# Norm factors folded into the split operands, side work paced by operand readiness, and the last two heads split on chip, in a two-layer hybrid decoder step

## The chip, the core and the metric

The kernel runs on one core of a Trainium2 chip. The metric is device time in microseconds, the median of three runs; lower is better. Durations in the text come from one profiled execution of the kernel before. Its engines are written as in the profile: PE (matrix products; PEld its weight loads), DVE (VectorE), ACT (ScalarE), POOL (GpSimd) and SP (which issues the weight loads from memory).

## The reference, cut to what matters

One inference step of two layers over 560 columns of tokens (16 meta tokens, 512 prompt tokens, 8 samples of 4 tokens), model width 1024. Each layer is a token mixer and a gated feed-forward part.

```python
h = rmsnorm(x, g_pre_mix)               # x * r * g, r = rsqrt(mean(x*x) + eps): one factor per token
z = h @ w_in                            # one projection into u | xb | gb | q | k | v | gc | gates a, b, c
y_a = s5_mixer(u)                       # complex diagonal scan, gelu, GLU
y_b = rglru_mixer(xb, gb)               # conv, block gates, linear scan, times gelu(gb)
y_c = retention_mixer(q, k, v, gc)      # 8 heads, rotary q and k, chunked decay, norm per head, times silu(gc)
m = sigmoid(ga) * (y_a @ w_branch_a) + sigmoid(gb) * (y_b @ w_branch_b) + sigmoid(gc) * (y_c @ w_branch_c)
x = x + rmsnorm(m @ w_out, g_post_mix)
h = rmsnorm(x, g_pre_ffn)
g, u = split(h @ ffn_w_up)
x = x + rmsnorm((gelu(causal_conv(g)) * u) @ ffn_w_down, g_post_ffn)
```

All is float32. The norm's factor r is one number per token, so it may be multiplied into h or into each product that h has been through.

## The kernel before, in words

**Products.** Activations stand transposed: 128 rows of a feature block by 560 token columns, in two column halves of 280 (`HS`). Each operand is held as a pair, a rounded part (`hi`) and the remainder (`lo`), and a product is three matmuls per block of 128 rows: hi·hi, hi·lo, lo·hi (`half`). A weight chunk of 128 output features is eight blocks: 24 matmuls per half, 48 per chunk. Weights come by SP from memory as `wr`, ACT casts them to `wh`, DVE subtracts for `wl`.

**The norm, deferred.** The split operands `hh`/`hl` (the list `hs`) hold x·g without r. r (`rn`, `N["r"]`) is ready only later, so every product is scaled when its PSUM tile is read: `by_column` (a DVE multiply by `rn`) for u, xb, gb, gc and the gates ta, tb, tc; the rotary tables `cosT` and `sinT` (tile `cst`) are multiplied by `rn` instead of k and q; v has its tokens on the partitions and is scaled by `rtok` on ACT. For gb, gc and the gates the multiply is done in place in PSUM and ACT reads the result.

**Order of the work.** The program writes its own order. A main line of weight chunks runs on PE: u and k, then per pair of heads `hp` q, v, gc and the units xb, gb of the LRU branch, then six gates tc, then the product bc of the heads' outputs, and so on. Beside it run generators of side work (S5, LRU, retention `ret_gen`, loads with splitting `load_split`), whose instructions are slipped into the main line by `pump` in the middle and at the end of each half, when a clock kept by the program (`clk`, class `Paced`) says that they are due; `finish` drains one generator before the main line goes on. The engines execute in order, so an instruction slipped in too early blocks what is queued behind it. All activations share 46 tiles of 128 x 560 (`slot`, `NG`), and a generator goes on only if enough are free.

**The end of retention.** Each head's output is stored to memory (`ycd`) on POOL's queue by `ret_gen`. Before the product bc, the main line drains the last pair of heads, then starts `load_split` over all eight heads (load as `y`, cast to `yh` on ACT, remainder `yl` on DVE) and drains it:

```python
box = [gate("tc") for _ in range(NTC)]
flush()
finish(ret, "ret")
yl = start(load_split(ycd, ych, 0.5))
finish(yl, "yl")
```

POOL issues all DMAs but the weights' and a few at the start. It also does small powers (`le`, `dt`, `E` of the preparation of S5 and LRU; `rn` of retention's norm) and memsets.

Of the kernel before, what the change touches and what calls it, by code (L numbers as in the profile page):

```python
# [18 lines left out]
D = 1024  # L19
# [63 lines left out]

@with_exitstack
def tile_hybrid_decoder(ctx: ExitStack, tc: tile.TileContext, I, O, cfg=None):
# [4 lines left out]
    clk = dict(V=0.0, A=0.0, G=0.0, P=0.0, D=0.0, set=None, used=0.0)  # L90
    SETS = {AF.Tanh: (1, 2), AF.Exp: (3, 1), AF.Gelu_apprx_tanh: (2,), AF.Ln: (3,), AF.Sqrt: (4,)}

    class Paced:
# [5 lines left out]
        def __getattr__(self, name):  # L99
            f, key = getattr(self.engine, name), self.key  # L100

            def call(out, *a, **k):
                if name == "preload_act_table_set":
                    if clk["set"] != 3:
                        clk["set"] = 3
                        clk["A"] = max(clk["A"], clk["P"]) + 1.3
                        f(out)
                    return
                n = 1
                for d in out.shape[1:]:  # L110
                    n *= d
                if key == "P":
                    src = k["rhs"] if name == "matmul" else out
                    clk["P"] += n * (0.42e-3 if src.dtype == FR else 1.7e-3) + 0.005
                elif key == "D":
                    clk["used"] = max(clk["used"], max(clk["P"], clk["V"], clk["A"]) + 2.5)
                else:
                    if key == "A":
                        c = 0.1 + n * 0.83e-3
                        if name == "activation":  # L120
                            t = SETS.get(a[1], ())
                            if t and clk["set"] not in t:
                                c += 1.3
                                clk["set"] = t[0]
                    elif key == "V":
                        c = 0.07 + n * (6.4e-3 if name == "reciprocal" else 1.04e-3)
                    else:
                        c = 0.1 + n * (165e-3 if k.get("op") == OP.pow else 1e-3)
                    clk[key] = max(clk[key], clk["P"]) + c
                    clk["used"] = max(clk["used"], clk[key])  # L130
                return f(out, *a, **k)  # L131
            return call

    V, A, G, P, SP, SQ = (Paced(e, k) for e, k in ((nc.vector, "V"), (nc.scalar, "A"), (nc.gpsimd, "G"), (nc.tensor, "P"), (nc.sync, "D"),
                                                  (nc.gpsimd, "D")))
# [27 lines left out]
    def pad_tile(name):  # L163
        return gen.tile([128, 592], FT, name=nm(name), tag="pad", bufs=3)

    def main_ps():
        return pm.tile([128, 512], FT, name=nm("pm"), tag="m", bufs=4)

    def side_ps(tag="x"):
        return pm.tile([128, 512], FT, name=nm("px"), tag=tag, bufs=2)  # L170
# [67 lines left out]
    def issue_raw(upto):  # L238
        while st["raw"] <= min(upto, len(chunks) - 1):
            i = st["raw"]  # L240
            src = chunks[i][1]
            n = src.shape[-1]
            if NRAW <= i < NRAW + BOOT:
                raws[i] = [(slot("wr")[:, :512], slice(o, o + 512)) for o in (0, 512)]
            else:
                raws[i] = [(ring.tile([128, 1024], FT, name=f"wr{i}", tag="raw", bufs=NRAW)[:, :n], slice(0, n))]
            for t, sl in raws[i]:
                SP.dma_start(t, src[:, sl])
            st["land"] = landed[i] = max(max(clk["P"], clk["V"]) + 3.8, st["land"] + 2.0)
            st["raw"] += 1  # L250
# [8 lines left out]
    def issue_hi():  # L259
# [10 lines left out]
        hi = pool.tile([128, 1024], FR, name=f"wh{i}", tag="hi" + x, bufs=b)  # L270
        lo = pool.tile([128, 1024], FR, name=f"wl{i}", tag="lo" + x, bufs=b)
# [37 lines left out]
    side = []  # L309

    SLACK, DEEP, SHALLOW = cfg.get("slack", 0.6), cfg.get("deep", 6.0), cfg.get("shallow", 1.0)
# [26 lines left out]

    def pump():
# [10 lines left out]
        for s in sorted([s for s in side if not s[4]], key=lambda s: s[2]):  # L350
            if (s in side and s[1] <= clk["P"] and used["n"] + s[3] <= NG
                    and max(clk["V"], clk["A"]) - clk["P"] < (st["shallow"] if s[2] else DEEP)):
                step(s)

    def force(but=None):

        for s in sorted(side, key=lambda s: (s[2], s[1])):
            if s is not but and used["n"] + s[3] <= NG:
                step(s)
                return  # L360
        assert False, ("no room", used["n"])

    def room(n):
        while used["n"] + n > NG:
            assert not used["side"]
            force()

    def finish(s, what=""):
        if cfg.get("verbose"):
            print("finish", what, s in side, "chunk", st["next"], "t", clk["P"], clk["V"], clk["A"], used["n"], flush=True)  # L370
        while s in side:
            t = min((t for t in side if t is s or t[2] and s[2]), key=lambda t: t[1])
            clk["P"] = max(clk["P"], t[1])
            if used["n"] + t[3] > NG:
                force(t)
# [271 lines left out]
    def by_column(N, h, out, ps, cols=None):  # L647

        until(N, "ready", h)
# [147 lines left out]
    def s5_gen(l, sp, p, ud, zd, qt):  # L797
# [162 lines left out]
        for n in range(12):  # L960
# [40 lines left out]
            for j, t in enumerate((hr, hi)):  # L1001
                G.memset(k3(t)[:, :, 8:9], 0.0)
# [153 lines left out]
    def ret_gen(l, hp, T, ycd, rp, before):  # L1156
# [172 lines left out]
        for h in range(2):  # L1329
# [10 lines left out]
            yield 0  # L1340
            SQ.dma_start(ycd[hd], sg)
            drop()
# [45 lines left out]
    def k_or_q(T, n, hs):  # L1388
        def ev(h, ps):
            if n not in T:  # L1390
                T[n] = slot(n + "f")
            A.copy(T[n][:, HS[h]], ps)
        return (n, lambda: hs, ev, None)

    def first_units(N, ud, T, between, lead):

        us = u_units(N, ud) + [k_or_q(T, "k", N["hs"])]
# [89 lines left out]
    for l in range(depth):  # L1487
# [3 lines left out]
        with ExitStack() as ph:  # L1491
            sp = ph.enter_context(tc.tile_pool(name=f"s5p{l}", bufs=1))

            def hslot(name):
                return sp.tile([128, 288], FT, name=nm(name), tag="q", bufs=NQ)
# [21 lines left out]
            for t in (cosT, sinT):  # L1517
                tt(t, t, N["r"])
# [8 lines left out]
            def lru_units(j):  # L1527
# [11 lines left out]
                unit("xb", hs, lambda h, ps: pad_evac(xp, ps, h, 3, N), go)  # L1539
# [9 lines left out]
            nl = 0  # L1549
            for hp in range(4):  # L1550
                T = TT[l] if hp == 0 else {}
                in_turn([k_or_q(T, n, hs) for n in ("k", "q") if n not in T])
                (i0, w0), (i1, w1) = weights("v"), weights("v")
                flush()
                ret = start(ret_gen(l, hp, T, ycd, rp, ret))
                T["v"] = []
                for c0 in (0, 2, 4):
                    ps = main_ps()
                    for c in range(c0, min(c0 + 2, 5)):
# [11 lines left out]
                        if c % 2 == 1 or c == 4:  # L1571
                            def ev(ps=ps, c0=c0, c1=c, T=T):
                                T["v"].append(slot("v"))
                                for i in range(c1 - c0 + 1):
# [7 lines left out]
                T["sg"] = []  # L1582
                for h2 in range(2):
                    box = {}

                    def ev(h, ps, box=box):
# [6 lines left out]
                    unit("gc", hs, ev, lambda T=T, box=box: T["sg"].append(box["t"]))  # L1593
# [4 lines left out]
            def gate(n, new=slot):  # L1598
                box = {}

                def ev(h, ps):
# [5 lines left out]
                    by_column(N, h, ps, ps)  # L1607
# [8 lines left out]
            def load_split(srcs, out, scale=None):  # L1616
                for src in srcs:
                    yield 3
                    t = slot("y")
                    SQ.dma_start(t, src)  # L1620
                    yield 2
                    a, b = slot("yh", FR), slot("yl", FR)
# [4 lines left out]
            st["shallow"] = cfg.get("sh1", 6.0)  # L1627
# [46 lines left out]
        with ExitStack() as ph:  # L1674
# [63 lines left out]
            drop(17)  # L1738
# [4 lines left out]
        with ExitStack() as ph:  # L1743
# [4 lines left out]
            if not last:  # L1748
                SQ.dma_start(cst[:, CO["cos"][0]:CO["cos"][0] + 2 * NT], I["cst"][:, CO["cos"][0]:CO["cos"][0] + 2 * NT])
# [329 lines left out]
```

## Time and profile before

| | before |
|---|---|
| median of 3 runs | 2341.22 us (2339.77 to 2342.35) |
| the profiled execution | 2338.64 us, span 2336.9 us, mean granted clock 0.99 |
| PE busy | 2273.8 us (97%), 17880 matmuls |
| DVE busy | 1664.4 us (71%) |
| ACT busy | 937.3 us (40%) |
| POOL busy | 317.6 us (14%) |

The profiled execution's own time is a little above its span, because the span runs from the first to the last instruction. A table by stages gives for each engine the microseconds it was busy; what is missing to the length of the stage is idle time. PEclk is the granted share of TensorE's full 2.4 GHz. A wait is put down to the instruction that released it.

### The profile page before, as it was taken

Reading aid. Unit: us, or ns where it says so; the run is one execution under the profiler, and the core shown is the slowest. Engines: PE = TensorE matmul, PEld = TensorE weight load, DVE = VectorE, ACT = ScalarE, POOL = GpSimd, SP = SyncE. Lnnn points to the kernel's source line nnn. Section 1 sums busy time; section 2 is a strip of 40 time slices with the busy share of each in tenths; the row PEclk is TensorE's granted clock in tenths of the full one; section 3 lists DMA queues with packets and bytes.
Section 4 is the critical chain, followed back from the end, with each engine's and each line's share of the span. In section 5 each row is a group of like instructions: output and inputs, shape, how many; then the busy total and the mean of one; then the engine's idle time right before and its main releaser. Section 6 shows DMA issues by size and latency. Waiting matters only on the chain.

```text
span 2336.9 us, 44994 instructions
## 1 busy us (share of the span) xinstructions
PE 2273.8 (97%) x17880; PEld 2253.0 (96%) x17880; DVE 1664.4 (71%) x4025; ACT 937.3 (40%) x2035; POOL 317.6 (14%) x585
## 2 busy tenths in 40 slices
PE   8999998999999999999999999979999999999997
PEld 7999998999999999999999999979999999999997
DVE  7888999887466845555588889888874667455555
ACT  4255536443435432223333455464434354332231
POOL 2222112011110000000241322110111100000011
PEclk9999999999999999999999999989999999999998
DMA  5333334233344332223342333332334433322331
GB/s 192 110 106 110 100 92 132 90 108 97 111 125 132 95 106 82 88 85 90 116 129 91 115 117 95 92 121 91 107 90 116 125 123 99 111 88 85 91 108 55
DMA packets 76707, 246.35 MB, mean 105 GB/s; under 512 B 13712, under 2 KB 16656, under 8 KB 76496
## 3 DMA queue, kind: packets, MB, share of 16 engines
q1 hardware_dynamic: 52704, 175.98, 25.0%
q0 software_dynamic: 23792, 67.49, 9.2%
q8 instruction: 141, 2.31, 0.4%
q14 instruction: 70, 0.57, 0.1%
HBM read 208.81 MB, written 29.76 MB: 102 GB/s over the span
## 4 chain that ended last, share of the span: by engine, by line
PE 65%; DVE 17%; issue 10%; ACT 4%; POOL 2%; DMA 2%; SPq 0%; POOLq 0%; DVEq 0%; ACTq 0%
PE pm L131 61%; PE px L131 4%; DVE wl L131 3%; DVE r L131 2%; ACT wh L131 1%; DVE ltr L131 1%; DVE pm L131 1%; DVE tg L131 1%; DVE cm L131 1%; POOL rn L131 1%; DVE sg L131 1%; DVE xc L131 1%; DMA wr<-in_wa 1%; DVE S L131 1%; DVE CA L131 1%
## 5 line engine op out<-in xcount | busy, mean ns | idle before, releaser
L131 ACT CAST wh<-wr 128x1024 fp32r<-128x1024 f32 (+3 forms) x347 | 347.3, 1004 | 509.9 <-PE pm L131 429.8
L131 DVE TENSOR_TENSOR wl<-wr,wh 128x1024 fp32r<-128x1024 f32 (+3 forms) x347 | 403.6, 1165 | 133.2 <-ACT wh L131 132.4
L131 PE MATMUL pm<-fh,wh 128*128 128x280 f32 (+2 forms) x1632 | 481.1, 295 | 10.4 <-ACT tg L131 4.5
L131 PE MATMUL pm<-mh,wh 128*128 128x280 f32 (+2 forms) x1664 | 483.2, 290 | 1.1 <-DVE gp L131 0.6
L131 PE MATMUL pm<-ml,wh 128*128 128x280 f32 (+2 forms) x1664 | 482.6, 290 | 0.0
L131 PE MATMUL pm<-mh,wl 128*128 128x280 f32 (+2 forms) x1664 | 482.1, 290 | 0.0
L131 PE MATMUL pm<-fh,wl 128*128 128x280 f32 (+2 forms) x1632 | 475.5, 291 | 0.0
L131 PE MATMUL pm<-fl,wh 128*128 128x280 f32 (+2 forms) x1632 | 475.4, 291 | 0.0
L131 PEld LDWEIGHTS pm<-fh,wh 128*128 128x128 f32 x1632 | 309.5, 190 | 12.9 <-ACT tg L131 4.8
L131 PEld LDWEIGHTS pm<-mh,wh 128*128 128x128 f32 x1664 | 313.1, 188 | 2.1 <-issue 0.9
L131 PEld LDWEIGHTS pm<-ml,wh 128*128 128x128 f32 x1664 | 312.7, 188 | 0.3
L131 PEld LDWEIGHTS pm<-mh,wl 128*128 128x128 f32 x1664 | 312.8, 188 | 0.0
L131 PEld LDWEIGHTS pm<-fl,wh 128*128 128x128 f32 x1632 | 309.4, 190 | 0.3
L131 PEld LDWEIGHTS pm<-fh,wl 128*128 128x128 f32 x1632 | 309.1, 189 | 0.0
L131 PE MATMUL pm<-hh,wh 128*128 128x280 f32 x928 | 276.1, 298 | 12.1 <-ACT hh L131 6.8
L131 PE MATMUL pm<-hh,wl 128*128 128x280 f32 x928 | 271.1, 292 | 1.3 <-DVE wl L131 1.3
L131 PE MATMUL pm<-hl,wh 128*128 128x280 f32 x928 | 271.3, 292 | 0.1
L131 PEld LDWEIGHTS pm<-hh,wh 128*128 128x128 f32 x928 | 175.3, 189 | 14.5 <-ACT hh L131 9.1
L131 PEld LDWEIGHTS pm<-hh,wl 128*128 128x128 f32 x928 | 175.4, 189 | 1.9 <-DVE wl L131 1.9
L131 PEld LDWEIGHTS pm<-hl,wh 128*128 128x128 f32 x928 | 175.0, 189 | 0.8 <-DVE hl L131 0.6
L131 PE MATMUL pm<-yh,wh 128*128 128x280 f32 (+2 forms) x448 | 133.9, 299 | 8.7 <-ACT yh L131 8.7
L131 PE MATMUL pm<-yl,wh 128*128 128x280 f32 (+2 forms) x448 | 131.5, 294 | 0.6 <-DVE yl L131 0.6
(363 smaller groups left out, 4229.3 us busy)
## 6 DMA issues: line engine op xcount, KB each, us to landing
wr<-in_wa SPq DMA_DIRECT2D x249, 512.0 KB, 3.6
wr<-in_w SPq DMA_DIRECT2D x44, 384.0 KB, 3.0
wr<-in_wd SPq DMA_DIRECT2D x32, 448.0 KB, 3.3
wr<-in_wd SPq DMA_DIRECT2D x16, 512.0 KB, 3.6
ycd<-sg POOLq DMA_DIRECT2D x16, 280.0 KB, 2.8
y<-ycd POOLq DMA_DIRECT2D x16, 280.0 KB, 5.4
ss<-in_rets POOLq DMA_DIRECT2D x16, 256.0 KB, 3.4
out_rets<-ss POOLq DMA_DIRECT2D x16, 256.0 KB, 2.6
```

Source lines behind the costliest of these rows:

```text
L131: return f(out, *a, **k)
```

## The change

1. **Norm factors into the operands.** A new generator `normalize` is started for each half as soon as r is known. For each of eight blocks POOL adds hi and lo into a spare tile and multiplies by r; when the products that still need the unscaled operands are past (`free[h]`), ACT casts the result into `hi` in place and DVE subtracts into `lo`. u, the first k, q, v and gc stay with unscaled operands. From the first LRU unit on, all PSUM tiles are read without the factor. The rotary tables are no longer scaled and no longer loaded again for the second layer.
2. **Pacing.** The program's clock now follows operands: each tile has the times at which it is made and last read, each instruction starts when its engine, its inputs and its output are free, and buffers that are reused carry their times over (`turn`, `cells`, `place`). The slack of a step falls from 0.6 to 0.3, the depth allowed in the gates' stretch from 6.0 to 3.0, and slots wanted by the pair of heads in work are reserved (`spare`).
3. **Heads.** The first six heads are loaded while the last pair is in work, up to three at a time; the last two are split where they are made, with no store and load.
4. A memset of two columns in S5 goes from POOL to DVE.

```diff
+                t = max(t, clk[e])
+                clk[e] = t + c
+                m[s] = t + c + lat
+                clk["used"] = max(clk["used"], t + c + lat)
...
+    def spare(s=None):
+        h = next((t for t in side if t in heads), None)
+        return h[3] if h is not None and h is not s else 0
...
     def by_column(N, h, out, ps, cols=None):
+        if N is None:
+            A.copy(out, ps)
+            return
...
-                G.memset(k3(t)[:, :, 8:9], 0.0)
+                V.memset(k3(t)[:, :, 8:9], 0.0)
...
-            yield 0
-            SQ.dma_start(ycd[hd], sg)
-            drop()
+            if straight is None:
+                yield 0
+                SQ.dma_start(ycd[hd], sg)
+                drop()
+            else:
+                yield 2
+                a, b = slot("yh", FR), slot("yl", FR)
+                split(sg, a, b, ALL, 0.5)
+                drop()
+                straight.append((a, b))
...
+    def normalize(N, h):
+        s, n = HS[h], wd(h)
+        while N["ready"] < h:
+            yield WAIT
+        yield 4
+        ts = [slot("nt") for _ in range(4)]
+        pair = [ts[k // 2][:, (k % 2) * H:(k % 2) * H + n] for k in range(8)]
+        for k in range(8):
+            hi, lo = (x[:, s].bitcast(FT) for x in N["hs"][k])
+            tt(pair[k], hi, lo, OP.add, G)
+            tt(pair[k], pair[k], N["r"][:, s], OP.mult, G)
+            yield 0
+        while not free[h]:
+            yield WAIT
+        for k in range(8):
+            hi, lo = (x[:, s] for x in N["hs"][k])
+            A.copy(hi, pair[k])
+            tt(lo, pair[k], hi.bitcast(FT), OP.subtract)
+        drop(4)
...
-            for t in (cosT, sinT):
-                tt(t, t, N["r"])
+            normed[:], free[:] = [start(normalize(N, h)) for h in range(2)], [False, False]
...
-                    by_column(N, h, ps, ps)
                     A.activation(X["g"][:, HS[h]], ps, AF.Gelu_apprx_tanh)
-                unit("gb", hs, ev, lambda: X.update(gb=X["g"]))
+                us = [("xb", lambda: hs, lambda h, ps: pad_evac(xp, ps, h, 3, None), go),
+                      ("gb", lambda: hs, ev, lambda: X.update(gb=X["g"]))]
+                if j:
+                    in_turn(us)
+                else:
+                    halves_apart(us, lambda: finish(normed[1], "norm"))
+                    drop()
...
+                if hp:
+                    in_turn(gcs)
+                else:
+                    halves_apart(gcs, lambda: free.__setitem__(0, True))
+                    free[1] = True
+                    finish(normed[0], "norm")
...
-                    by_column(N, h, ps, ps)
                     if n == "ta":
...
-            st["shallow"] = cfg.get("sh1", 6.0)
+            st["shallow"] = cfg.get("sh1", 3.0)
...
+            yl = start(load_split(ycd[:6], ych, 0.5, lambda i: rets[i // 2] not in side))
             finish(ret, "ret")
-            yl = start(load_split(ycd, ych, 0.5))
             finish(yl, "yl")
+            ych += ych_late
...
-            if not last:
-                SQ.dma_start(cst[:, CO["cos"][0]:CO["cos"][0] + 2 * NT], I["cst"][:, CO["cos"][0]:CO["cos"][0] + 2 * NT])
```

## Rows read from the trace of the kernel before

**Rows 1.** The page's head: busy time, share of the span and instructions of each engine.
```profile
PE 2273.8 (97%) x17880; PEld 2253.0 (96%) x17880; DVE 1664.4 (71%) x4025; ACT 937.3 (40%) x2035; POOL 317.6 (14%) x585
```
**Rows 2.** Busy time by stage: stretch, its length, engines (instructions), PEclk, DMA share, GB/s.
```profile
58.00:98.00 40.00, 40.00 (x332) 39.48 (x331) 33.36 (x91) 12.75 (x22) 10.08 (x22) 1.00 0.42 124
98.00:356.00 258.00, 257.06 (x2114) 252.54 (x2113) 229.34 (x640) 124.51 (x283) 57.35 (x102) 1.00 0.33 101
356.00:428.00 72.00, 64.45 (x471) 62.81 (x470) 64.79 (x156) 45.20 (x104) 11.09 (x24) 0.95 0.36 118
428.00:574.00 146.00, 144.63 (x1142) 144.26 (x1141) 123.19 (x323) 55.79 (x157) 13.06 (x34) 1.00 0.32 96
1160.00:1220.00 60.00, 54.42 (x389) 53.37 (x388) 50.22 (x137) 20.77 (x39) 22.82 (x27) 0.94 0.42 130
1220.00:1260.00 40.00, 40.00 (x330) 39.47 (x331) 36.67 (x98) 11.75 (x22) 9.99 (x22) 1.00 0.38 115
1260.00:1520.00 260.00, 257.83 (x2115) 252.91 (x2115) 228.70 (x636) 125.12 (x284) 58.49 (x102) 1.00 0.33 100
1520.00:1604.00 84.00, 70.53 (x515) 69.41 (x514) 73.08 (x181) 47.76 (x114) 11.37 (x26) 0.90 0.34 111
1604.00:1744.00 140.00, 138.37 (x1112) 138.00 (x1111) 116.10 (x299) 54.16 (x148) 12.86 (x32) 1.00 0.32 96
```
**Rows 3.** PE's waits, 355 to 430 us (first three) and 1520 to 1605 us (last three).
```profile
PE pm L131 <- ACT tg L131: 3.6, 2, 3.2
PE pm L131 <- ACT yh L131: 1.7, 1, 1.7
PE px L131 <- DVE hn L131: 1.1, 1, 1.1
...
PE pm L131 <- ACT yh L131: 7.1, 1, 7.1
PE pm L131 <- ACT tg L131: 4.5, 1, 4.5
PE px L131 <- DVE CA L131: 1.7, 2, 1.0
```
**Rows 4.** POOL and its DMA issues in order of time, second layer's end of retention.
```profile
1552.83 0.54 POOL L131 DMA_DIRECT2D ycd<-sg  x1
1558.15 2.69 POOL L131 DMA_DIRECT2D y<-ycd  x5
1570.23 0.54 POOL L131 DMA_DIRECT2D y<-ycd  x1 [7.74 <-DVE ltr L131]
1577.19 0.54 POOL L131 DMA_DIRECT2D y<-ycd  x1 [6.42 <-DVE yl L131]
```
**Rows 5.** DVE by group and form: busy us, mean ns, idle time before and its releaser.
```profile
L131 DVE TENSOR_TENSOR pm<-pm,rn 128x280 f32<-128x280 f32 x104 | 46.7, 452 | 26.1 <-PE pm L131 25.6
L131 DVE TENSOR_TENSOR pm<-pm,rn 128x276 f32<-128x276 f32 x24 | 10.8, 450 | 18.8 <-PE pm L131 18.7
L131 DVE TENSOR_TENSOR xp<-pm,rn 128x280 f32<-128x280 f32 x12 | 5.3, 445 | 0.3
L131 DVE TENSOR_TENSOR fl<-ga,fh 128x280 fp32r<-128x280 f32 x36 | 16.2, 451 | 22.2 <-ACT fh L131 22.2
```
**Rows 6.** ACT by group and form, columns as in rows 5.
```profile
L131 ACT CAST fh<-ga 128x280 fp32r<-128x280 f32 x36 | 15.3, 424 | 16.7 <-DVE ga L131 16.7
```
**Rows 7.** DVE in order of time, first layer: rotary tables, then the first LRU unit.
```profile
58.94 1.39 DVE L131 TENSOR_TENSOR cst<-cst,rn 128x560 f32<-128x560 f32 x2
...
97.90 0.44 DVE L131 TENSOR_TENSOR xp<-pm,rn 128x280 f32<-128x280 f32 x1
```
**Rows 8.** POOL by group and form, columns as in rows 5.
```profile
L131 POOL MEMSET S<- 128x256 f32 x8 | 2.2, 330 | 0.0
```
**Rows 9.** POOL and then DVE in order of time at one of retention's powers.
```profile
129.56 2.09 POOL L131 TENSOR_TENSOR rn<-rn,mhalf 112x10 f32<-112x10 f32 x1 [15.65 <-DVE rn L131]
...
130.47 0.26 DVE L131 TENSOR_TENSOR cm<-bbi,AR 128x96 f32<-128x96 f32 x1
```

More of the change, by code (lines that the diff above doesn't have):

```diff
@@ L245, in issue_raw @@
             else:
-                raws[i] = [(ring.tile([128, 1024], FT, name=f"wr{i}", tag="raw", bufs=NRAW)[:, :n], slice(0, n))]
+                raws[i] = [(turn(ring.tile([128, 1024], FT, name=f"wr{i}", tag="raw", bufs=NRAW), "raw", NRAW)[:, :n], slice(0, n))]
             for t, sl in raws[i]:
                 SP.dma_start(t, src[:, sl])
-            st["land"] = landed[i] = max(max(clk["P"], clk["V"]) + 3.8, st["land"] + 2.0)
+            landed[i] = max(made[t.tensor.name].max() for t, _ in raws[i])
             st["raw"] += 1
@@ L306, in release @@
         convs.pop(i)
-    side = []
-    SLACK, DEEP, SHALLOW = cfg.get("slack", 0.6), cfg.get("deep", 6.0), cfg.get("shallow", 1.0)
+    side, heads = [], []
+    SLACK, DEEP, SHALLOW = cfg.get("slack", 0.3), cfg.get("deep", 6.0), cfg.get("shallow", 1.0)
     WAIT = 100
@@ L350, in pump @@
         for s in sorted([s for s in side if not s[4]], key=lambda s: s[2]):
-            if (s in side and s[1] <= clk["P"] and used["n"] + s[3] <= NG
+            if (s in side and s[1] <= clk["P"] and used["n"] + s[3] + spare(s) <= NG
                     and max(clk["V"], clk["A"]) - clk["P"] < (st["shallow"] if s[2] else DEEP)):
@@ L357, in force, with room @@
         for s in sorted(side, key=lambda s: (s[2], s[1])):
-            if s is not but and used["n"] + s[3] <= NG:
+            if s is not but and used["n"] + s[3] + spare(s) <= NG:
                 step(s)
-                return
[L361 to L366, printed above, removed]
+                return True
+        return False
+    def room(n):
+        while used["n"] + n + (0 if used["side"] else spare()) > NG:
+            assert not used["side"]
+            clk["P"] += 0.05
+            if not force() and used["n"] + n <= NG:
+                return
     def finish(s, what=""):
@@ L1153, in lru_gen, with ret_gen @@
         drop()
-    def ret_gen(l, hp, T, ycd, rp, before):
+    def ret_gen(l, hp, T, ycd, rp, before, straight=None):
         kf, qf = T["k"], T["q"]
@@ L1494, in hslot @@
             def hslot(name):
-                return sp.tile([128, 288], FT, name=nm(name), tag="q", bufs=NQ)
+                return turn(sp.tile([128, 288], FT, name=nm(name), tag="q", bufs=NQ), "q", NQ)
             zd = [dram.tile([128, 4, 140], FT, name=f"zd{l}_{m}") for m in range(6)]
@@ L1614, in gate, with load_split @@
                 return box
[L1616 to L1620, printed above, removed]
+            def load_split(srcs, out, scale=None, there=lambda i: True):
+                on, i = [], 0
+                while on or i < len(srcs):
+                    while i < len(srcs) and len(on) < 3 and there(i) and used["n"] + 3 <= NG:
+                        on.append((slot("y"), clk["P"] + 4.5))
+                        SQ.dma_start(on[-1][0], srcs[i])
+                        i += 1
+                    if not on or clk["P"] < on[0][1]:
+                        yield 0 if on else 3
+                        continue
                     yield 2
+                    t = on.pop(0)[0]
                     a, b = slot("yh", FR), slot("yl", FR)
```

121 lines of the change are left out of this document (88 added, 33 removed).

## The prediction

> **What bounds the kernel now.** I read the head of the page first: PE is busy 97% of the span [rows 1]. The change removes and adds no matmul, so the 17880 of them stay, and only the time in which PE stands still or runs slowly can be won. Next the table by stages [rows 2]: the reader is to subtract the PE column from the length. In the feed-forward stretches little is missing. In the mixers (58 to 574 us, and 1220 to 1744 us for the second layer) two short stretches stand out, where the main line goes from the gates tc to the heads' product bc: 7.55 us idle at 356 to 428 and 13.47 us at 1520 to 1604, with PEclk at 0.95 and 0.90 where the neighbours have 1.00. Idle time alone understates the loss, since a slower clock lengthens what is busy. The counts give it whole: behind the first stretch 1142 matmuls take 144.63 us, 126.7 ns each; at that rate 471 matmuls need 59.7 us, and 72 were spent: 12.3 us lost. Behind the second, 138.37 us over 1112 is 124.4 ns; 515 need 64.1 of 84: 19.9 us lost. Together 32.2 us. The other six mixer rows (58 to 98, 98 to 356, 428 to 574 and their counterparts) are short of PE time by 0, 0.94, 1.37, 0, 2.17 and 1.63 us, 6.1 us in all. So 38.3 us is the most that this change can take away where it works.
>
> PE's waits in the two stretches name the causes [rows 3]: `tg`, a gate's PSUM tile that isn't read yet (3.6 + 4.5 = 8.1 us), `yh`, the split heads (1.7 + 7.1 = 8.8 us), and S5's operands (1.1 + 1.7 = 2.8 us). Those 19.7 us of waits stand for 32.2 us; the remaining 12.5 us fit the clock, (1 - 0.95) x 72 + (1 - 0.90) x 84 = 12.0 us. Spread in proportion, tg costs 13.2, yh 14.4 and S5 4.6 us.
>
> Last DVE: 33.4 + 229.3 + 64.8 + 123.2 = 450.7 us busy of 516 in the first layer's mixer, 87%, and 90% in the first bad stretch [rows 2]. It isn't PE's equal, but a gate waits in its queue behind bursts of S5 and LRU work.
>
> **The change, part by part.**
>
> *The factor leaves the PSUM reads.* DVE loses its in-place multiplies: there are three groups, the second layer's last of 272 columns like its 276: 46.7 + 10.8 + about 10.7 = 68.2 us for 152, of which eight for the first pair's gc stay (3.6 us): -64.6 us [rows 5]. The three groups of LRU reads (280, 248, 32 columns) go to ACT; the first is 5.3 us, and by columns the others come to about 7 more: -12 us. The tables' scaling goes: two layers of 1.39, -2.8 us [rows 7]. Added: 32 subtracts of 280 columns at 0.451, +14.4 us; eight multiplies for the first k and q, +3.6 us [rows 5]; 48 tiny memsets, under 0.1 us each, +4 us. DVE net: about -57 us, some 29 a layer, to 82% of the mixer. ACT gets 32 casts at 0.424 = 13.6 us [rows 6] and the LRU reads, about 11 us; at 40% busy [rows 1] it has room. What matters is the path: a gate's tile goes from PE to ACT straight, without DVE's queue. ACT is busy 45.2 of 72 and 47.8 of 84 us in the bad stretches [rows 2], so it can be late by a few casts, not by a burst. I take four fifths of 13.2: -10.6 us.
>
> *Heads.* In the second layer the last store `ycd` is issued at 1552.83, the first five loads at 1558.15, one more waits behind LRU's `ltr` until 1570.23, the last until 1577.19 behind a split that had to free its tiles [rows 4]. So it isn't the 2 to 5 us of a load that PE waits for, but the late issue of the last loads. With six loads instead of eight and the last pair split where it lies, those two issues go, and with them two stores and two loads a layer on POOL's queue. What is late next: the free tiles. Loads may start only while three tiles are free, and the pair in work reserves its own; if none come free before the drain, the six loads begin where they begin now. I take three quarters of 14.4: -10.8 us, with bounds of 0 and -14.4.
>
> *Pacing.* A side step is issued when its inputs should exist, so PE's short waits for S5 and retention shrink. But the slack halves, which pulls the other way. Half of S5's 4.6 and half of the 6.1 us elsewhere: -2.3 - 3.0 = -5.3 us; bounds +5 and -10.7.
>
> *The added work on POOL.* 32 adds and multiplies of 280 columns a layer, in order with POOL's DMA issues: behind them stand retention's partner copies `rs`, `qd`, `ss` and the LRU weights, whose lateness is covered by the many chunks until retention's last step. No row shows a POOL add. From below, a memset of 256 columns is 0.33 us [rows 8]; from above, a power of 10 columns takes 2.09 us [rows 9]. I take 0.8 us, nearer the memset, because an add passes three operands and the power's time is arithmetic: 25.6 us a layer. The stretch for it runs from where the tables were scaled, 58.9, to the first LRU unit's read at 97.9 [rows 7], and POOL is busy 10.1 us there [rows 2]: 29.9 us free, so it just fits; at 0.33 it is 10.6, at 2.09 it is 66.9 and 37 us late a layer. By the Trainium skill, GPSIMD Engine Reference, section 3.1 Elementwise, 2048 columns of such an add take 4497 ns, so 280 would be an estimated 0.61 us and 20 us a layer, which leaves the sum as it is.
>
> *The in-place casts and subtracts.* Each half's eight pairs must pass ACT and DVE (8 x 0.45 = 3.6 us) while PE does the other half of two chunks, 48 matmuls, some 6 us. That hides them if the queues are short. DVE has 36.7 of 40 us taken at 1220 to 1260, and gets 7.2 + 1.8 - 1.4 = 7.6 more, 4.3 us too many; in the first layer 33.4 + 7.6 is 1.0 too many [rows 2]. S5's preparation can be put off, so between 0 and 5.3 us show on PE. I take +3.
>
> *The sum:* -10.6 - 10.8 - 5.3 + 3.0 = -23.7 us. The profiled execution's own time is 2338.64 us, so 2314.9; the median of the runs is 2341.22, 2.6 above it, so 2317.5 us. Its own range is 2303 (all 38.3 us) to 2331.
>
> **The rivals.**
>
> *POOL and DVE keep each other out* (slower). Both work through the stretch from 58 to 98 us; if an add on POOL stops DVE's operations with two inputs in SBUF, or the reverse, the two share 40 us: DVE 33.4 + 7.6, POOL's 25.6, is 66.6, 26.6 too many; some of DVE's reads are of PSUM and S5 can be put off, so I count 20 a layer: 2317.5 - 3 + 40 = 2355 us. It decides against the change from about 13 us lateness a layer, that is from about 1.3 us for a POOL operation. Against it: at 129.56 us POOL runs a power that reads SBUF, and inside its 2.09 us DVE's multiplies of two SBUF operands keep 0.26 us [rows 9]. But that power reads 10 columns only. The Trainium skill, SBUF — State Buffer, section Who interferes with whom, says that a DVE instruction with two SBUF inputs and a GpSimd instruction that reads SBUF contend, the second fully blocked until the first ends. By that rule this rival would come out; the trace's one overlap doesn't show a whole instruction blocked.
>
> *The loads stay late.* If tiles are short, the heads' part is worth nothing and only the gates' part and pacing remain: 2341.2 - 10.6 - 5.3 + 3 = 2328 us. For it: the present loads wait for tiles [rows 4]. Against it: two fewer are needed.
>
> *More than that.* With DVE at 82%, all 38.3 us go and the change of layers (5.58 us idle and a clock of 0.94 over 60 us [rows 2]) is paced better by some 5: 2341.2 - 43 = 2298 us.
>
> *Nothing comes of it.* The reserve of tiles and the shallow depth hold S5 back, and its drain before the last gates becomes PE's wait; or the operands cost what the gates save: some 24 us back, 2341 us. Against it: the stretches that hold that drain are short of only 1.37 and 1.63 us now [rows 2], and S5 gets DVE time.
>
> **How the numbers follow.** Forecast 0.45, loads stay late 0.14, more than that 0.15, nothing 0.11, slower 0.15. A measurement of this kernel tells 0.2%, about 4.7 us, from no change. The first three are faster, with a little of them lost to the middle: 0.73; same 0.11; slower 0.16. The range for 8 in 10 goes from the larger gain to the middle case's far end: 2296 to 2347 us; the slower rival beyond it is left out. The likeliest case's own range is 2303 to 2331.
>
> **What would show it.** After the change the two transition stretches should run at clock 1.00 with at most 4 us idle each, no wait for `tg`, and the heads' casts spread over the tc gates. DVE should be near 1607 us busy and POOL near 317.6 + 51 - 6 = 363 us. Right at the first LRU unit of each layer PE should wait less than 3 us for `hh` or `hl`. The prediction is wrong if PE stands still there for 10 us, if POOL's adds take over 1.3 us, if DVE's operations beside them grow longer, or if PE still waits for `yh`.

## The result and the profile after

The changed kernel takes 2364.01 us (2362.0 to 2368.96), the kernel before beside it 2340.49: a ratio of 1.0104 [1.0085, 1.0123]. It is 1% slower where a gain of 1% was forecast, and beyond the range's 2347. Its profiled execution took 2362.0 us with a span of 2360.2, 23.3 more than before.

The head of the page answers [rows 1]:
```profile
PE 2275.2 (96%) x17880; PEld 2252.6 (95%) x17880; DVE 1645.1 (70%) x3929; ACT 957.6 (41%) x2088; POOL 364.4 (15%) x592
```
DVE's work fell by 19.3 us, where the change had been priced at -57. The table by stage answers [rows 2], with the same columns; the stretches that begin at 371 us lie 15 us later than before, those from 1548 on 28 us later. That is how much later the main product comes that stood at the end of each bad stretch (428 and 1604 us); the ones at their starts come 11.5 and 36.8 us later, so the stretches hold nearly the same work and not exactly the same.
```profile
58.00:98.00 40.00, 25.92 (x214) 25.68 (x212) 39.11 (x70) 7.71 (x11) 35.27 (x47) 0.85 0.25 75
98.00:112.00 14.00, 14.00 (x92) 14.00 (x93) 12.27 (x31) 5.84 (x14) 6.04 (x15) 0.82 0.40 125
371.00:443.00 72.00, 64.09 (x489) 63.14 (x489) 58.51 (x158) 42.31 (x100) 11.17 (x17) 0.95 0.32 99
443.00:589.00 146.00, 142.99 (x1127) 142.59 (x1127) 116.97 (x320) 56.55 (x158) 26.58 (x49) 1.00 0.37 110
1262.00:1290.00 28.00, 14.28 (x90) 14.06 (x91) 25.01 (x48) 5.83 (x14) 15.34 (x20) 0.70 0.25 73
1548.00:1632.00 84.00, 76.74 (x591) 75.66 (x590) 72.62 (x196) 49.11 (x119) 14.23 (x22) 0.96 0.32 103
1632.00:1772.00 140.00, 137.50 (x1101) 137.31 (x1101) 101.52 (x266) 50.31 (x130) 23.84 (x44) 1.00 0.37 109
```
The first row and its counterpart at 1262 hold the loss: from 58 to 98 us PE was busy for all 40 us, and now for 25.92, while DVE is full, 39.11 us with 70 instructions where it had 33.36 with 91. PE in order of time shows one stop in each layer and what follows it:
```profile
97.89 0.60 PE L190 MATMUL pm<-hh,wl 128*128 128x280 f32 x1 [14.08 <-DVE wl L190]
98.29 0.44 PE L190 MATMUL pm<-hh,wh 128*128 128x280 f32 x1
98.52 0.44 PE L190 MATMUL pm<-hl,wh 128*128 128x280 f32 x1
...
1275.21 0.60 PE L190 MATMUL pm<-fh,wl 128*128 128x280 f32 x1 [13.51 <-DVE wl L190]
```
PE stands for 14 us for the low half of a weight of gc, which DVE splits; then matmuls start 0.23 us apart instead of 0.127, TensorE's lower level of 1.2 GHz (the granted share is 0.50 from 97.8 to 101 us, and 1.00 again from 105 on). Counting PE's main products, which are the same 15984 in every kernel here, gives each stage's time from its first product to the next stage's: gc of the first head pair takes 29.6 and 29.1 us (layers 1 and 2), where it took 14.1 and 13.6. That is +31.0; all other stages together are 7.7 us shorter.

DVE in order of time just ahead of the first stop:
```profile
80.96 1.16 DVE L190 TENSOR_TENSOR bbr<-bre,cr 128x384 f32<-128x384 f32 x1
...
87.32 0.93 DVE L190 TENSOR_SCALAR cin<-cin 128x384 f32<-128x384 f32 x1
88.21 0.08 DVE L190 MEMSET tBr<- 128x24 f32 x1
...
92.22 0.82 DVE L190 TENSOR_TENSOR tBr<-tBr,bt 128x48 f32<-128x48 f32 x1
...
96.62 1.22 DVE L190 TENSOR_TENSOR wl<-wr,wh 128x1024 fp32r<-128x1024 f32 x1
97.75 0.25 DVE L190 TENSOR_TENSOR tBr<-tBr,sc 128x96 f32<-128x96 f32 x1
```
In the kernel before, the same instructions took:
```profile
80.33 0.55 DVE L131 TENSOR_TENSOR bbr<-bre,cr 128x384 f32<-128x384 f32 x1
84.53 0.35 DVE L131 TENSOR_SCALAR cin<-cin 128x384 f32<-128x384 f32 x1
92.00 0.21 DVE L131 TENSOR_TENSOR tBr<-tBr,bt 128x48 f32<-128x48 f32 x1
```
POOL beside it in the changed kernel, with two of the three groups of its added work, which answer [rows 8] (the third, the second layer's adds, has a mean of 945 ns):
```profile
92.20 0.77 POOL L190 TENSOR_TENSOR nt<-nt,rn 128x280 f32<-128x280 f32 x1
...
L190 POOL TENSOR_TENSOR nt<-nt,rn 128x280 f32<-128x280 f32 x32 | 29.1, 909 | 2.5
L190 POOL TENSOR_TENSOR nt<-hh,hl 128x280 f32<-128x280 f32 x16 | 15.1, 946 | 0.0
```
S5's preparation and POOL's adds hold each other up: a multiply of 384 columns takes 1.16 us instead of 0.55, one of 48 columns 0.82 instead of 0.21, about as long as the add beside it. Behind POOL's last add (94.55) 96 columns take 0.25. The split `wl` that PE waits for stands in DVE's queue behind all of that.

In the stretches from tc to bc PE now waits (371 to 443 us, then 1548 to 1632 us; answers [rows 3]):
```profile
PE pm L190 <- ACT yh L190: 4.4, 1, 4.4
PE px L190 <- DVE z L190: 2.3, 1, 2.3
...
PE pm L190 <- ACT yh L190: 4.5, 1, 4.5
PE px L190 <- DVE hn L190: 1.9, 1, 1.9
```
`tg` is gone. By the prediction's own method 10.0 us are lost in the first stretch (489 matmuls at 126.9 ns are 62.0 of 72) and 10.2 in the second (591 at 124.9 ns are 73.8 of 84): 20.2 in place of 32.2. The forecast was a clock of 1.00 with at most 4 us idle in each; the clock is 0.95 and 0.96, and 7.9 and 7.3 us are idle. POOL's issues ahead of the second (answers [rows 4]):
```profile
1594.81 0.56 POOL L190 DMA_DIRECT2D zd<-z  x1 [23.98 <-ACT z L190]
1596.05 0.54 POOL L190 DMA_DIRECT2D yd<-ltr  x1 [0.69 <-DVE ltr L190]
1596.58 3.18 POOL L190 DMA_DIRECT2D y<-ycd  x6
```

### The profile page after: what moved, and what is told of

Its sections match the earlier page's. It is cut to its first block, busy times and chain, and to the rows that moved or that the text cites. A ratio compares the mean times of both kernels' runs of the same rounds, so it can differ in the third digit from the quotient of the medians.

```text
span 2360.2 us, 44863 instructions
## 1 busy us (share of the span) xinstructions
PE 2275.2 (96%) x17880; PEld 2252.6 (95%) x17880; DVE 1645.1 (70%) x3929; ACT 957.6 (41%) x2088; POOL 364.4 (15%) x592
## 4 chain that ended last, share of the span: by engine, by line
PE 73%; DVE 12%; issue 9%; ACT 2%; POOL 2%; DMA 1%; SPq 0%; DVEq 0%; POOLq 0%; ACTq 0%
PE pm L190 67%; PE px L190 6%; DVE wl L190 2%; DVE sc L190 1%; ACT wh L190 1%; DVE r L190 1%; DVE fo L190 1%; DMA y<-ycd 1%; DVE sums L190 1%; DVE xc L190 0%; DVE part L190 0%; DVE ga L190 0%; DMA wr<-in_wa 0%; POOL out_y L190 0%; DVE S L190 0%
## 5 line engine op out<-in xcount | busy, mean ns | idle before, releaser
L190 PEld LDWEIGHTS pm<-hh,wh 128*128 128x128 f32 x928 | 176.6, 190 | 10.7 <-ACT hh L190 9.1
```

## The experiments

Theory: POOL's adds and DVE hold each other up at the start of a layer, and nothing else is wrong. Its rivals: the new pacing loses time; the casts, or the adds' place in POOL's queue, are at fault.

### The parts alone and together

One part undone (`e1`: the norm as before), the pacing alone (`e8`), the heads alone (`e13`), the pacing undone (`e4`). The reservation of tiles (`spare`, in `pump`, `room` and `finish`) belongs to the pacing, but it stays in all of these, in `e4` and `e13` too; what "old pacing" means below is the old clock with its slack and depth:
```diff
 e1:  -normed[:], free[:] = [start(normalize(N, h)) for h in range(2)], [False, False]
      +for t in (cosT, sinT): tt(t, t, N["r"])            # and by_column at xb, gb, gc, gates
 e8:  e1, and load_split(ycd, ych, 0.5) as before, no ych_late
 e13: the kernel before with load_split(ycd[:6], ...), ych_late, spare and V.memset
 e4:  class Paced, SLACK 0.6, sh1 6.0 as before; spare stays
```


> The changed kernel with its first part undone: r is multiplied at each PSUM read again, no adds and multiplies on POOL, tables scaled and reloaded. Theory A (POOL's 64 operations and DVE's operations with two SBUF inputs keep each other out, so wl is late and PE stands 14.3 and 13.7 us): both stops go, with the slow clock behind them some 31 us, and DVE's 57 us of extra multiplies come back as they were in the kernel before: 2325 to 2338 us. Theory B (the new pacing issues side work too early and so blocks wl): the two stops stay in some form, 2355 us or more. Theory C (the in-place casts and the halves' order make PE wait): also about 2330, told apart from A by the next two kernels.

> The changed kernel with its first and third parts undone: only the new pacing (and the memset moved to DVE) stays. With the factors undone alone the kernel was at 2356.8 us, 17 us over the kernel before. Theory P (the new pacing issues PE's side matmuls before their operands are there, and they hold up PE's queue): most of the 17 us stays, 2350 to 2362 us. Theory H (the loss is the heads' part: the new loads, up to three at a time, stand in POOL's in-order queue behind S5's store and in front of ACT's and DVE's work): within 5 us of the kernel before, 2335 to 2345 us.

> The kernel before with the change's third part alone: the last two heads of y are split from SBUF, the other six loads start as their heads end, three in flight; old pacing, the norm as before. Theory A (the prediction's step: three quarters of the 14.4 us of waits for yh go): 2328-2332. Rival B (the wait for yh only moves: the loads are issued behind a store in POOL's in-order queue that waits for the LRU's work, and what was 7 us late is late by about as much): 2337-2343, with 8-14 us of waits for yh left.

> The changed kernel with the pacing of the kernel before (clock, slack 0.6, depth 6.0); norm factors by POOL and heads on chip stay. Theory A (POOL and DVE keep each other out) alone: the two stops of 14 us stay, 2355 to 2370 us. Theory P beside it: the stops stay, but some 10 to 17 us of the other waits go, 2343 to 2354 us.

Measured: `e1` 2356.82 us (1.0072 [1.0057, 1.0087]), `e8` 2357.69 (1.0074 [1.0059, 1.0089]), `e13` 2338.34 (0.9997 [0.9988, 1.0005]), `e4` 2367.28 (1.0114 [1.0099, 1.0129]). So the theory falls as the only cause: the pacing alone costs 17.7 us, the heads alone bring nothing, and the norm adds 7.2 on top of both. `e8` came out by its theory P, `e13` by its rival B, `e4` by its theory A. `e1` came out by none: both stops are gone (gc takes 14.1 and 13.6 us again), and most of the loss stays. The parts don't add up one by one either: undone in the changed kernel (`e4`), the new pacing gives back nothing, 3.3 us more are lost, and gc still takes 26.7 and 26.4 us. The pacing's loss is no single stop. `e8` shows its longest one (columns as in [rows 2]):
```profile
PE px L190 <- DVE hn L190: 19.7, 3, 8.5
...
490.00:500.00 10.00, 9.79 (x78) 9.56 (x76) 3.69 (x7) 4.92 (x11) 3.40 (x7) 1.00 0.80 227
500.00:509.00 9.00, 0.67 (x3) 0.70 (x4) 8.82 (x24) 4.20 (x13) 0.00 (x0) 0.71 0.17 49
509.00:515.00 6.00, 6.00 (x31) 6.00 (x31) 5.84 (x21) 2.26 (x9) 0.55 (x1) 0.58 0.04 16
```
An S5 product stands at the head of PE's queue, main products behind it, and waits 8.5 us for `hn`; the clock then is 0.58 for 6 us more.

In `e13` six loads go out together, late, behind the stores and loads of S5 in POOL's order:
```profile
1561.58 0.54 POOL L135 DMA_DIRECT2D zd<-z  x1 [36.73 <-ACT z L135]
1566.50 0.54 POOL L135 DMA_DIRECT2D yd<-ltr  x1 [4.38 <-issue]
1567.08 2.20 POOL L135 DMA_DIRECT2D V<-ud  x4
1569.28 3.36 POOL L135 DMA_DIRECT2D y<-ycd  x6
```
Before, the first five went at 1558.15 and the last at 1577.19 [rows 4]. The waits for `yh` fall from 8.7 to 6.6 us over the kernel, those for `z` are new with 5.2, and `tg` stays at 8.1.

### POOL beside DVE

`e3` is the kernel before with the 64 POOL operations added, whose results nothing reads; `e7` puts as much POOL time there that only writes; `e2` does the change's adds on DVE; `e6` is the changed kernel with S5's preparation held back until the pairs are written:
```diff
 e3: +nc.gpsimd.tensor_tensor(dmy, hi, lo, op=OP.add)
     +nc.gpsimd.tensor_tensor(dmy, dmy, N["r"][:, s], op=OP.mult)
 e7: +nc.gpsimd.memset(dmy, 0.0)                          # 448 columns, four in place of the two
 e2: -tt(pair[k], hi, lo, OP.add, G)                      # and the multiply
     +tt(pair[k], hi, lo, OP.add)
 e6: +while any(s in side for s in normed): yield 0       # ahead of each step of s5_prep
```


> The kernel before, with the same 64 POOL adds and multiplies of 280 columns put in at the same place, reading the operands and r, writing a tile that nothing reads; nothing waits for them and the order of the rest is that of the kernel before. Theory A: DVE's operations beside them stretch as in the changed kernel, and PE stops for wl by 8 to 14 us a layer: 2358 to 2372 us. Theories B and C: nothing depends on them, within 5 us of the kernel before, 2336 to 2346 us.

> The kernel before, with POOL memsets of 448 columns (128 in all, four where the other dummy has an add and a multiply, about 0.49 us each, so some 63 us of POOL in the same stretches), which write SBUF and read nothing. If any busy POOL holds DVE up, or POOL's late DMA issues are the cause: 2355 to 2370 us. If it is POOL's reading that keeps DVE's second input out: within 6 us of the kernel before.

> The changed kernel with the 64 adds and multiplies on DVE instead of POOL; all else as in the changed kernel. DVE gets 64 x 0.45 = 29 us more. Theory A: DVE's operations in the 40 us after the tables' place return to their lengths of the kernel before (384 columns 0.55 us, not 1.1), DVE needs about 33 + 6 + 14 us there, the stops shrink from 14 to 3 to 8 us each: 2338 to 2350 us. Theory C (order of halves and the in-place chain): the stops stay near 14 us each or grow, 2360 to 2375 us.

> The changed kernel, with the S5 preparation of a layer held back until the normalised pairs of the layer are written, so that POOL's adds and multiplies run beside fewer VectorE instructions. Theory A (POOL's reads and VectorE's two-operand instructions of the S5 preparation hold each other up, and that alone delays the weight split in front of the gc products): POOL's adds fall from 0.91 to about 0.7 us, the two stops of 14 us for the low half of a weight fall under 5 us each, and the time falls from 2364 to 2340-2350, less whatever the later preparation costs. Rival B (the adds are this long beside any VectorE work, the weight splits themselves included): the adds stay at 0.85 us or more, the stops stay above 9 us, 2358-2370. Rival C (the conflict goes, but the S5 units now wait for their preparation): the stops are gone and the waits stand at the first S5 units instead, 2355-2375.

Measured: `e3` 2378.52 us (1.0166 [1.0151, 1.0181]), `e7` 2362.99 in one run, `e2` 2348.32 (1.0034 [1.0022, 1.0045]), `e6` 2349.09 (1.0044 [1.003, 1.0058]). `e3` and `e7` keep PE's order of the kernel before, instruction by instruction, and POOL is as busy in both. `e3` is above the range of its theory A; `e7` took as long as its first alternative, by POOL's late issues and not by DVE. First `e3`, then `e7`: the page's head and the weight splits from 58 to 125 us.
```profile
PE 2284.0 (96%) x17880; PEld 2261.8 (95%) x17880; DVE 1697.2 (71%) x4025; ACT 937.4 (39%) x2035; POOL 379.4 (16%) x649
L131 DVE TENSOR_TENSOR wl<-wr,wh 128x1024 fp32r<-128x1024 f32 x8 | 10.9, 1364 | 0.0
```
```profile
PE 2279.1 (97%) x17880; PEld 2257.7 (96%) x17880; DVE 1666.3 (71%) x4025; ACT 936.8 (40%) x2035; POOL 378.8 (16%) x713
L131 DVE TENSOR_TENSOR wl<-wr,wh 128x1024 fp32r<-128x1024 f32 x8 | 9.8, 1220 | 0.7 <-ACT wh L131 0.7
83.78 1.98 POOL L131 DMA_DIRECT2D rs<-kf  x4
```
Work that only writes leaves DVE where it was (1664.4 us before); work that reads costs it 31 us more, and the kernel 15.5. The other 23 of `e3`'s 39 us, which `e7` has too, come with a second effect: retention's copies `rs` are issued at 83.78 instead of 60.55 (`e7`), behind the added work in POOL's queue, and PE waits 16.6 us for `kf`. So the adds' place in POOL's queue can cost time; in the changed kernel it doesn't show, where the copies are issued at 72.61 and PE has no wait for `kf`. The Trainium skill, SBUF — State Buffer, section Who interferes with whom, says that a DVE instruction with two SBUF inputs contends with a GpSimd instruction that reads SBUF, not with one that only writes. These two runs agree: in the first layer a product of two SBUF tiles of 264 columns keeps 0.43 us beside `e7`'s memsets and takes 0.90 to 1.03 beside `e3`'s adds. Work that only writes isn't free for every form, though: a TENSOR_SCALAR of 264 columns, with one input, takes 0.30 us before, 0.50 in `e7` and 0.69 in `e3` (means of five).

In the changed kernel itself, POOL against DVE is worth 2364.01 - 2348.32 = 15.7 us (under the old pacing, `e4` against `e9` below, 25.4); the order of the side work differs in both pairs, so these two numbers are less clean than `e3` against `e7`. `e6` takes the stops away, 58 to 98 us and 1262 to 1290 us:
```profile
58.00:98.00 40.00, 36.37 (x288) 35.30 (x287) 29.60 (x33) 12.14 (x22) 38.81 (x48) 1.00 0.35 111
...
1262.00:1290.00 28.00, 25.47 (x184) 23.50 (x183) 24.17 (x47) 14.00 (x34) 14.96 (x19) 0.94 0.28 84
```
gc is back at 12.9 and 13.9 us. But the adds did not fall to 0.7 us as its theory A expected; they grew. DVE and POOL from 66 us on, with POOL's group from 55 to 130 us:
```profile
66.53 0.43 DVE L190 TENSOR_TENSOR qf<-pm,rn 128x280 f32<-128x280 f32 x1
66.89 1.44 DVE L190 TENSOR_TENSOR wl<-wr,wh 128x1024 fp32r<-128x1024 f32 x1
...
67.20 1.77 POOL L190 TENSOR_TENSOR nt<-hh,hl 128x280 f32<-128x280 f32 x1
...
L190 POOL TENSOR_TENSOR nt<-hh,hl 128x280 f32<-128x280 f32 x16 | 17.5, 1096 | 0.0
```
So the two engines still hold each other up. I take each DVE instruction beside the adds, less the median of the same instruction in the kernel before and in `e2`: in the changed kernel 33 and 34 instructions a layer are longer, by 16.5 and 17.3 us in all; in `e6` 22 and 20, by 12.9 and 10.5. One that meets an add is some 0.5 us longer, whether it has up to 96 columns (14 of 32 in the first layer, 0.53 us each) or 264 to 384 (17 of 25, 0.52). Holding the preparation takes a third of the conflict away, no more; the stop goes because the preparation no longer stands in DVE's queue in front of the split. A multiply of PSUM by `rn` (`qf`, one SBUF input) keeps its 0.43 us beside an add. What `e6` does not give back is the pacing, and pairs that come late: the first layer's adds end at 99.9 us instead of 94.6, PE waits for `hl`, `fh` and `fl` in xb and gb, and these take 19.1 and 18.5 us, 5.5 and 3.7 more than in the changed kernel.

### The adds on DVE, under the old pacing and elsewhere

`e9` is `e2` with the old pacing, `e15` that without the heads, `e10` is `e2` with the loads of `y` on SP's queue, `e18` is `e6` and `e19` is `e9` with the hold, both in the old pacing:
```diff
 e10: -SQ.dma_start(on[-1][0], srcs[i])
      +SP.dma_start(on[-1][0], srcs[i])
```


> The changed kernel with the adds and multiplies on DVE (2348.3 us with the new pacing) and the pacing of the kernel before. Theory P: 2325 to 2338 us, faster than the kernel before. Theory H: pacing doesn't matter, 2344 to 2352 us.

> The kernel before with the change's first part alone, its adds and multiplies on VectorE instead of POOL; old pacing, heads as before. The adds and multiplies on VectorE are 128 of about 0.35 us, some 45 us in place of some 68 us of multiplies by column that go. Theory A (the prediction's gates step is right and only POOL was the wrong engine for the adds): the tg waits in front of the gates go and 2328-2336. Rival B (what the gates gain is given back at the start of a layer, where the adds and casts stand between weight splits): the stages xb to gc lose 8-14 us over both layers and the total is 2338-2346.

> The changed kernel with the adds and multiplies on DVE (2348.3 us), and the loads y of the heads and of LRU issued on SP's queue and not on POOL's. If these loads are late because they stand in POOL's queue behind S5's store that waits for z: PE's waits for yh (4.4 and 4.5 us in the changed kernel) go with the slow clock behind them, 2334 to 2342 us. If free tiles or the program's order hold them: within 4 us of 2348. SP's queue also carries the weights and waits for their buffers; if that holds the loads up, slower than 2350.

> The changed kernel with the S5 preparation held back until the normalised pairs are written, and the old pacing. Theory A (the two causes add up: holding is worth 15 us and the pacing some 15): 2330-2342, the stops for the low half of a weight gone. Rival B (under the old pacing the adds meet other VectorE work, as in the run with the old pacing alone at 2367): 2348-2362. Rival C (the held preparation makes the S5 units late, since the old pacing lets it run further ahead and so loses more by the hold): 2343-2355 with waits in hp1 to lru4,5.

> The adds and multiplies on VectorE, the S5 preparation held back until they are done, the old pacing, and the late heads split on chip. Without the hold it took as long as the kernel before (2341.9 us), and lost 4.6 and 4.3 us in the gc and xb stages of the first layer. Theory A (VectorE had too much to do there, and the hold takes the preparation's share out): those stages go back to within 2 us of the kernel before and the time to 2332-2338. Rival B (the preparation is as late as it was early and the loss moves to hp1 to lru4,5): 2338-2348.

Measured: `e9` 2341.88 us (1.0009 [1.0, 1.0018]), `e15` 2345.06 (1.003 [1.002, 1.004]), `e10` 2360.75 (1.0086 [1.0069, 1.0103]), `e18` 2351.21 (1.0053 [1.0038, 1.0068]), `e19` 2354.23 (1.0063 [1.0047, 1.008]). `e15` came out by its rival B, `e18` where its rivals B and C overlap, `e9` between its two theories. (The adds and multiplies are 64 of 0.45 us, not the 128 of 0.35 in the expectation of `e15`.) `e15` loses 8.9 us in gc and xb, gb of the first layer, 1.1 in the second, and gains 14.7 in the tc gates of both, which other stages give back. In xb and gb of the first layer PE now waits for the normalised pairs `hh` and `hl`: 5.7 us in `e2`, 6.5 in `e9`. Holding the preparation helps where POOL does the adds (`e4` to `e18`, 16 us) and hurts where DVE does (`e9` to `e19`, 12 us), against the expectation of `e19`; with the old pacing it adds nothing to `e6`, against that of `e18`. `e10` was a miss: with the same order on PE it is 12 us worse than `e2`, 6 of them in the last stage, behind the last store's issue, and why is open. The heads' loads go out later from SP's queue (415.5 for 405.9 us, 1580.3 for 1576.3), and PE's waits for `yh` are 5.0 us where `e2` has 2.4. No version beats the kernel before; `e13` equals it, and `e9` is 1.9 us from it.

### Which part of the pacing

The lead alone put back (`e11`), lead and slack both (`e16`: only the model is new, with `spare`), the constants alone (`e17`: only the model is old), and the kernel before with the slack moved by 0.05 us:
```diff
 e11: e8 with cfg.get("sh1", 6.0)
 e16: e8 with cfg.get("sh1", 6.0), cfg.get("slack", 0.6)
 e17: the kernel before with cfg.get("sh1", 3.0), cfg.get("slack", 0.3)
 e20: the kernel before with cfg.get("slack", 0.55)
 e21: the kernel before with cfg.get("slack", 0.65)
```


> The new pacing alone (2357.7 us), with the lead that low-priority side work may have in the later stages put back from 3.0 to 6.0 us. Theory A (the smaller lead is what makes y, hn and the sums late): the waits for hn and yh fall from 27 us to under 15, and the time to 2343-2350. Rival B (it is the model of when an operand is ready that moves side work later or bunches it, whatever the lead): less than 4 us of change, 2354-2361.

> The new pacing alone with both constants of before (slack 0.6, lead 6.0) in its new model of readiness. With slack 0.3 it took 2357.7 us at lead 3.0 and 2365.9 us at lead 6.0. Theory A (the new model itself lets side work go out in an order that makes later steps late, whatever the constants): 2354-2370. Rival B (the halved slack lets side work in front of weight splits and evacuations that are not ready, and the model is harmless): 2338-2348.

> The kernel before with the two constants alone (slack 0.3 in place of 0.6, lead 3.0 in place of 6.0), its old model kept. Theory A (the new model is the cause, and the constants only fit it): the old model, which counts every operation as ready once its engine's clock passes it, loses little, 2334-2346. Rival B (the constants are the cause): 2350-2362.

> The kernel before with the slack at 0.55 us in place of 0.6, nothing else; the order of the side work changes from hp1 of the first layer on. Theory A (the order of the kernel before is one that happens to fit; others lose whatever moves them): 2345-2362, much like the runs with the new model or the new constants. Rival B (slack and lead act by their size: 0.3 and 3.0 together gave +23 us): a twelfth of that or less, 2337-2341.

> The kernel before with the slack at 0.65 us in place of 0.6, nothing else. Theory A (any other order loses): 2345-2362, on the same side as the step down. Rival B (the slack acts by its size): 2334-2341, and on the other side from the step down.

Measured: `e11` 2365.88 us (1.0118 [1.0105, 1.0132]), `e16` 2355.69 (1.0072 [1.0057, 1.0087]), `e17` 2362.14 (1.01 [1.0085, 1.0116]), `e20` 2356.68 (1.0077 [1.0061, 1.0094]), `e21` 2352.68 (1.0063 [1.0048, 1.0078]). The model alone, the constants alone, and a step of 0.05 us either way all cost 14 to 28 us. `e16`, `e20` and `e21` came out by their theory A, `e17` at the edge of its rival B; `e11` by neither, since the old lead costs the new model 8 us more. What the five share is a new order. Of the 1896 side products on PE, so many stand within three main products of where they stood before:
```
kernel   share   time against before
e13      0.94    no difference
e21      0.41    +14 us
e20      0.27    +18
e11, e8  0.18, 0.17    +28, +18
e16      0.12    +17
e17      0.09    +23
e9, e15  0.04, 0.04    +2, +7
```
The last line is of kernels that also have the norm's work moved. It says that a new order doesn't have to lose, and that the share doesn't tell how much it loses.

In `e20` the second layer's stretch from tc to bc and the one behind it answer [rows 2] (PE, clock, DMA share, GB/s): the first has fewer matmuls than before, and the next, where the clock was 1.00, has lost some too.
```profile
1520.00:1604.00 84.00, 67.74 (x485) 0.88 0.31 99
1604.00:1744.00 140.00, 134.16 (x1065) 0.98 0.30 93
```

## Why the prediction was wrong

*Pacing* is one of two steps that failed: "-2.3 - 3.0 = -5.3 us; bounds +5 and -10.7". Alone it is +17.7, outside its bounds. I priced the waits that a better model could shorten, and not that each operation's place changes: every other order of the same work that was tried costs 14 to 28 us, and the new model has no better one to offer than a slack moved by 0.05 us. That a new order is enough to lose this much is shown (`e20`, `e21`); what makes the order of before better isn't, nor whether it had been picked as the best of many. The waits fall on whatever side operand comes late (`hn`, `yh`, `W`, `z`), each with some us of low clock behind it.

*The added work on POOL* is the other, and in the changed kernel the larger: "I take 0.8 us ... so it just fits". The size was right for an add alone (0.77 us) and not far off on average (0.91 to 0.95); POOL's 364.4 us busy are what was forecast. What failed is the overlap, put at nothing, and with it the test on which the slower rival was put aside, one power of 10 columns beside DVE [rows 9]. That rival, *POOL and DVE keep each other out*, is what happens in the gc stage. It had 20 us a layer; the gc stages show 15.5 each, and DVE is busy 38 us longer than the forecast 1607. The stop came at gc, ahead of the first LRU unit where I had looked for one, and for `wl`. The Trainium skill's sentence quoted under it spoke against the change and was right; a measured row of a much smaller operation was no counter-proof. The Trainium skill's other figure (GPSIMD Engine Reference, section 3.1 Elementwise, an estimated 0.61 us) came out too short: an add took 0.77 us at best.

*Heads*, "three quarters of 14.4", brought nothing: `e13` has no difference, and 8.9 us of waits for `yh` are left in the changed kernel's two stretches, where 8.8 were [rows 3]. The rival *the loads stay late* named the result; whether for its reason, short tiles, isn't shown. In POOL's order the loads come behind S5's `zd<-z`, which waits 24 us for its data in the changed kernel and 37 in `e13`. That this place makes them late isn't shown either: taken off POOL's queue in `e10` they went out later than in `e2`, from a queue that they share with the weights. The cause stays open.

*The factor leaves the PSUM reads* held where it was aimed: `tg` no longer stops PE in the two stretches, which lose 12.0 us less. `e15`, the norm alone with its adds on DVE, gains 14.7 us in the gates. Between two kernels with the new pacing, the same change gains 8.5 us (`e1` to `e2`), against -10.6 + 3 forecast; only 0.10 of the side products keep their place there, so part of that may be the order. Against the order of before it shows as a loss, +6.9 in `e15`.

*The in-place casts and subtracts* held in size, 425 and 442 ns each, and by luck in effect: PE has no stop of 3 us for `hh` or `hl` at the first LRU unit, but it has just stood 14 us at gc. Where that stop is gone, it waits 5.7 us (`e2`) and 6.5 us (`e9`) for the pairs in the first layer alone, more than the 3 of both layers.

Along one chain of runs the differences are: pacing +17.7, heads on it -0.9, norm on both -8.5, POOL in place of DVE +15.7: 24.0 us, which is 2364.0 less 2340. They add up because each starts where the last one ends, and not because the causes are independent: by another chain the pacing costs 6.4 us with the adds on DVE (`e9` to `e2`) and nothing with them on POOL (`e4`). By stages of the changed kernel, gc's +31.0 is more than the whole loss.

## What to carry to other kernels

Where a program's order is computed from a model of time, an edit to the model is an edit to every queue: measure the scatter first, with two meaningless small steps of a constant, and price a change of pacing by that scatter and not by the waits it aims at; a difference between two orders that is no larger than the scatter isn't the price of a cause. Before work is moved to POOL, list the DVE instructions with two SBUF operands in the same stretch and count them: here each one that met a POOL add was some 0.5 us longer, however few columns it had. Look also at the DMAs that POOL issues: work put in front of them makes them late, as `rs` was by 23 us in `e7`.

## What the runs showed of the hardware

Beside POOL's adds, from 77 to 94.6 us of the changed kernel, 12 of 20 DVE instructions of two inputs and 24 or 48 columns took 0.6 to 0.8 us, and eight kept their 0.2. An instruction with a single SBUF operand isn't safe in every form: `cin`, a TENSOR_SCALAR of 384 columns, took 0.93 us in place of 0.35. POOL pays too: an add of 0.77 us took 1.77 beside a weight split of 1024 columns (`e6`). After a stop of 14 us matmuls came 0.23 us apart, and the clock averaged 0.82 over the next 14 us.
